# Two half tiles of the output projection moved into the last sample pass, and the sample's loads put in the order of their use

## The chip, the cores and the metric

The kernel runs on one core of a Trainium2 chip, as one program. The metric is the time of one execution on the device in microseconds (us). Before the change it was timed in three runs: 1134.77, 1136.65 and 1139.01, median 1136.65. One more execution was profiled; the times of the views are counted from the start of its span.

## The reference, cut to what matters

One layer of a hybrid decoder works on 512 prompt tokens and 64 sample tokens (8 sequences of 8 new tokens each, with 2048 tokens of past in paged caches). All 576 tokens share the weights.

```python
o_a = nsa(...)    # sparse attention; for the sample: compressed, 16 selected 64-token blocks, window
o_b = hgrn2(...)  # gated linear recurrence
m = ma * (o_a @ w_branch[:512]) + mb * (o_b @ w_branch[512:])   # the merge
x = x + m @ w_out                                               # the output projection
h = rms_norm(x); a, b = split(h @ ffn_w_in); x = x + (silu(conv(a)) * b) @ ffn_w_out
```

`ma` and `mb` are sigmoid gates of 1024 columns each. Everything is float32. The kernel splits each operand of its large products into a high part of fewer bits and the rest (`split`: a cast on ScalarE, a subtraction on VectorE or GpSimd) and adds three products (high by high, high by rest, rest by high), so a weight tile of 128 x 1024 costs 24 matmuls for each half of the tokens. A half is 288 columns (`HF`): the first holds prompt tokens 0 to 287, the second the other prompt tokens and the 64 sample tokens.

## The kernel before, in words

The stages follow each other in `main`: the recurrence and the projections, then `prompt` (attention of the prompt, the gates and the part of the merge that comes from `o_b`), then `sample`, `merge`, `out_proj` and `ffn`. The program is traced in this order and a scheduler gives every engine its own instructions in a fixed order; `issue_after` ties an instruction behind another of its engine. An engine executes its queue in that order and waits at an instruction whose operands aren't there. Tiles of one `tag` share a few buffers, and a load into a buffer waits until the tile before it has been read.

`sample` goes over the 8 sequences in four passes of two (`pr` 0 to 3). A pass needs 32 pages of the cache, 128 KB each: four "halves" of 8 pages (`half`), two for each sequence. Ten buffers hold halves (`NS`), so halves 10 to 15 reuse buffers of earlier ones. A pass also needs a window of keys (`wk`, 512 KB) and one of values (`wv`, 512 KB); four buffers with the tag `nraw` hold these. All these loads, and the loads of weights, stand in the queue of SyncE (SP). The addresses of the pages are read from a table, 8 at a time, and each page is a DMA of its own.

In the code, a pass does the scores of the new keys and the window (`scores_new`, L1569), the exponentials on ScalarE (`softmax_cached`, `softmax_window`), two tiles of the merge's first half (`fill("A")`, `merge_half`, below), the transposes of the probabilities to keys by queries (`by_key`; the copies out of PSUM are ScalarE's for even and VectorE's for odd quarters, L1616 and L1618), the products with the values (`av`, L1624), of which the window's are the last, and then the sum `t1`, its transpose (L1699) and the copies into `oa` (L1704). The next pass's scores (`scores`, L1548) lie between. Loads stand in the program where their buffer comes free: halves 10 and 11 after the second quarter of pass 0, halves 12 and 13 after the fourth, then the values' window of pass 1 (L1677) and the keys' window of pass 2 (L1679).

`merge_half(d)` makes tile `d` (128 of the 1024 columns) of the merge for the first half of the tokens: it loads the gates (`zm`, from the DRAM tile `gbd`, on GpSimd's queue) and the weight `wBr` (SP's queue), splits the weight, runs 12 matmuls (L1346), multiplies and adds on VectorE (L1347) and GpSimd (L1348), and stores the result to `gbd` on GpSimd's queue (L1349). Passes 0 to 3 run tiles 0 and 1, 2 and 3, 4 and 5, 6 and 7. The loads of a pair of tiles stand behind the merges of the pair before, and their splits (`prepare`) behind `t1` of the pass before, ahead of its copies into `oa`.

`merge` loads the eight stored tiles of the first half again (`mb`), splits them into `m`, starts the first output tile with its first half (`begin_out(0)`: 24 matmuls, L1746), splits `oa` into `oas`, and for each of eight tiles loads the gates (`tm`), splits a weight, runs 12 matmuls (L1736) for the second half, multiplies, adds and splits the result into `m` (L1737, L1738, L1739). Then comes the first half of output tile 1 (`begin_out(1)`). `out_proj` runs the second half of these two tiles (L1746) and the other six whole (`gemm`, L378).

## Time and profile before

| | us |
|---|---|
| median of three runs | 1136.65 (1134.77 to 1139.01) |
| the profiled execution, its own time | 1137.31 |
| its span, first to last instruction | 1135.6 |
| TensorE busy | 1072.9 |
| VectorE busy | 745.9 |
| GpSimd busy | 517.1 |
| ScalarE busy | 487.6 |
| mean granted clock of TensorE | 0.978 |

The execution's own time is 1.7 us above its span. PE is TensorE's matmul, PEld its weight load, DVE VectorE, ACT ScalarE, POOL GpSimd, SP SyncE. Matmuls are pipelined, so a busy PE need not be at its peak; the time between the starts of equal matmuls tells their cost. [...] A wait is put down to what ended it last. The sample lies between some 547 and 648 us of the span, the merge between 649 and 683, the whole output tiles behind that.

### The profile page before, as it was taken

The page shows a single profiled execution, that of the slowest core. Times are in us where ns is not written, and L with a number is a line of the kernel's source. Part 1 is how long each engine was busy: PE and PEld are TensorE (multiplying, and loading weights), DVE is VectorE, ACT ScalarE, POOL GpSimd, SP SyncE. Part 2 cuts the span into 40 slices and gives each one's busy share as a digit, 9 for nine tenths or more (in the row PEclk, how much of TensorE's full clock was granted, in tenths as well). Part 3 has the DMA queues.
Part 4 walks back from the last instruction along what each step waited for, and adds up shares of the span by engine and source line. Part 5 has one row for each costly group of instructions (what it writes and reads, how often), then busy time and mean ns, then how long its engine had stood idle before and what let it go on. Part 6 is the DMA issues. An engine that isn't in the chain of part 4 may idle for free.

```text
span 1135.6 us, 21797 instructions
## 1 busy us (share of the span) xinstructions
PE 1072.9 (94%) x7968; PEld 1012.2 (89%) x7968; DVE 745.9 (66%) x1322; ACT 487.6 (43%) x1015; POOL 517.1 (46%) x590
## 2 busy tenths in 40 slices
PE   6999999999999899999985799999999999999998
PEld 5988889898999899989753589999999999999997
DVE  6667665674267757897632484576877868677783
ACT  5523443443444467776522444433343324333341
POOL 3663623832365444333220264354566645554553
PEclk8999999999999899999996999999999999999999
DMA  5633556454341331173688576422364314643223
GB/s 192 184 110 124 158 167 196 127 156 150 113 159 59 127 93 59 53 243 111 218 277 266 184 268 198 123 69 63 115 216 124 101 40 135 210 120 93 69 75 125
DMA packets 106957, 160.98 MB, mean 142 GB/s; under 512 B 11745, under 2 KB 68834, under 8 KB 106722
## 3 DMA queue, kind: packets, MB, share of 16 engines
q1 hardware_dynamic: 105394, 155.40, 43.9%
q0 software_dynamic: 1024, 3.54, 1.0%
q8 instruction: 63, 1.03, 0.4%
q10 hardware_dynamic: 432, 0.65, 0.2%
q14 instruction: 44, 0.36, 0.1%
HBM read 136.34 MB, written 27.33 MB: 144 GB/s over the span
## 4 chain that ended last, share of the span: by engine, by line
PE 45%; DVE 11%; DMA 4%; POOL 4%; issue 3%; SPq 2%; ACT 2%; DVEq 0%; POOLq 0%; ACTq 0%
PE ps_g L378 25%; PE ps_g L1854 7%; PE ps_g L1213 2%; PE ps_po L1624 2%; DVE w L327 2%; PE ps_hp L1320 1%; SPq L943 1%; PE ps_sb L1312 1%; PE ps_sa L1280 1%; POOL rr L1141 1%; DVE r L1151 1%; PE ps_sc L1548 1%; DVE wsp L327 1%; PE ps_tr L1613 1%; DVE g L327 1%
## 5 line engine op out<-in xcount | busy, mean ns | idle before, releaser
L378 PE MATMUL ps_g<-h,w 128*128 128x288 f32 x2112 | 281.0, 294 | 0.0
L378 PEld LDWEIGHTS ps_g<-h,w 128*128 128x128 f32 x2112 | 279.9, 188 | 0.1
L378 PE MATMUL ps_g<-xg,wsp 128*128 128x288 f32 x1200 | 184.1, 306 | 16.0 <-ACT wsp L326 9.3
L378 PEld LDWEIGHTS ps_g<-xg,wsp 128*128 128x128 f32 x1200 | 169.0, 194 | 22.4 <-ACT wsp L326 9.5
L326 ACT CAST w<-wraw 128x512 fp32r<-128x512 f32 (+1 forms) x140 | 84.3, 609 | 141.7 <-PE ps_g L378 98.6
L1854 PE MATMUL ps_g<-g,w 128*128 128x288 f32 x924 | 126.1, 296 | 4.7 <-DVE vv L1887 3.1
L1854 PEld LDWEIGHTS ps_g<-g,w 128*128 128x128 f32 x924 | 123.3, 188 | 6.6 <-DVE vv L1887 4.0
L327 POOL TENSOR_TENSOR w<-wraw,w 128x512 fp32r<-128x512 f32 (+1 forms) x58 | 80.8, 1397 | 52.7 <-ACT w L326 50.3
L327 DVE TENSOR_TENSOR w<-wraw,w 128x512 fp32r<-128x512 f32 (+1 forms) x82 | 76.3, 932 | 23.2 <-ACT w L326 19.6
L326 ACT CAST wsp<-wraw 128x1024 fp32r<-128x1024 f32 (+2 forms) x66 | 58.0, 893 | 62.2 <-DMA wraw<-in_wBr 21.2
L327 DVE TENSOR_TENSOR wsp<-wraw,wsp 128x1024 fp32r<-128x1024 f32 (+2 forms) x43 | 57.0, 1328 | 23.9 <-ACT wsp L326 22.3
L327 POOL TENSOR_TENSOR wsp<-wraw,wsp 128x1024 fp32r<-128x1024 f32 (+2 forms) x23 | 46.9, 2039 | 56.3 <-ACT wsp L326 56.3
L541 PE MATMUL ps_t<-wsp,xg 128*128 128x262 f32 (+1 forms) x480 | 60.9, 286 | 0.0
L541 PEld LDWEIGHTS ps_t<-wsp,xg 128*128 128x128 f32 x480 | 58.9, 189 | 0.1
L1168 POOL TENSOR_TENSOR zg<-zg,rsb 128x576 f32<-128x576 f32 x16 | 25.7, 1606 | 58.4 <-ACT zg L1167 58.4
L916 PE MATMUL ps_pc<-phi,w 128*128 128x256 f32 x256 | 50.8, 289 | 0.0
L326 ACT CAST phi<-praw 128x2048 fp32r<-128x2048 f32 x16 | 30.4, 1901 | 47.4 <-PE ps_pc L916 30.4
L327 DVE TENSOR_TENSOR plo<-praw,phi 128x2048 fp32r<-128x2048 f32 x14 | 32.7, 2338 | 22.2 <-ACT phi L326 14.2
L326 ACT CAST w<-wsum 128x512 fp32r<-128x512 f32 (+1 forms) x48 | 27.7, 584 | 44.6 <-PE ps_g L378 19.8
L327 DVE TENSOR_TENSOR w<-wsum,w 128x512 fp32r<-128x512 f32 (+1 forms) x48 | 41.9, 875 | 6.4 <-ACT w L326 6.1
L1964 POOL TENSOR_TENSOR Y<-Y,rs 128x576 f32<-128x576 f32 x22 | 32.2, 1464 | 25.8 <-ACT Y L1963 25.6
L916 PEld LDWEIGHTS ps_pc<-phi,w 128*128 128x128 f32 x256 | 41.7, 194 | 0.8 <-issue 0.8
(444 smaller groups left out, 2145.0 us busy)
## 6 DMA issues: line engine op xcount, KB each, us to landing
wraw<-in_wFi SPq DMA_DIRECT2D x44, 512.0 KB
praw<-in_pc SPq DMA_DIRECT2D x256, 64.0 KB
praw<-in_pkv SPq DMA_DIRECT2D x96, 128.0 KB
wraw<-in_wM SPq DMA_DIRECT2D x16, 512.0 KB
wraw<-in_wFo SPq DMA_DIRECT2D x16, 512.0 KB
gbd<-zg SPq DMA_DIRECT2D x24, 288.0 KB
wraw<-in_wBr SPq DMA_DIRECT2D x24, 256.0 KB
x<-in_xT SPq DMA_DIRECT2D x16, 288.0 KB
```

The lines of the kernel that those rows point to most:

```text
L326: self.copied = nc.scalar.copy(hi, src)
L327: (eng or nc.vector).tensor_tensor(lo, src, hi.bitcast(F32), op=ALU.subtract)
L378: self.last = nc.tensor.matmul(ps[:, h, 0:HF], w[wk // 4][:, cw, wk % 4] if isinstance(w, list) else w[:, cw, wk, :], (x[cx] if isinstance ...
L541: nc.tensor.matmul(ps[:, 0:n], self.xg[cx][:, k, j * 128:j * 128 + 128], w[k][:, cw], start=(k == 0 and c == 0), stop=(k == KT - 1 and c = ...
L916: self.nc.tensor.matmul(ps, self.w1[:, cw, j, k], x[cx][:, k], start=start and k == 0 and n == 0, stop=k == 7 and n == 2, skip_group_check ...
L943: self.page_dma = nc.sync.dma_start(raw[:, i], dram[bass.ds(rv[i], 1)].rearrange("o p c -> p (o c)"))
L1141: nc.gpsimd.tensor_tensor(rr[0:r, 0:nh], ss[0:r, 0:nh], self.mhalf[0:r, 0:nh], op=ALU.pow)
L1168: nc.gpsimd.tensor_tensor(z, z, self.rsb, op=ALU.mult)
L1213: self.last = nc.tensor.matmul(ps, w[:, cw, k], self.obs[cx][:, k, c], start=n == 0, stop=n == 11)
L1624: self.last = self.nc.tensor.matmul(s.po[64 * bb:64 * bb + 64, branch], pt[:, 64 * bb:64 * bb + 64], v[bb], start=s.first[bb], stop=False, ...
L1854: self.last = nc.tensor.matmul(ps, w[:, cw, j], g[j][:, cx, x], start=first and j == 0 and (cw, cx) == (0, 0), stop=j == m - 1 and (cw, cx ...
L1964: nc.gpsimd.tensor_tensor(s, s, self.rs2, op=ALU.mult)
```

## The change

The diff does the following.

- In `sample`, halves 6 and 7 are loaded, then the values' window of pass 1, then halves 8 and 9. In the passes, the keys' window of pass `pr` + 2 is loaded behind the second quarter and its halves (in pass 0 ahead of halves 12 and 13), and the values' window of pass `pr` + 2 behind the last product of pass `pr`.
- In pass 3, `early_m` takes over four page buffers and one new tile: for `m`'s first half (eight tiles, `mf`) and the weights of output tiles 0 and 1 (`wf`), which are loaded into two window buffers and split on ScalarE and GpSimd. Tiles 0 to 5 of `m` are loaded from `gbd` into the buffer of an earlier pass's scores and split after the second quarter; tiles 6 and 7 are split from the result of `merge_half` in SBUF.
- `begin_out(0)` stands behind the last product of pass 3, `begin_out(1)` behind the transpose of its `t1`. Each copies its PSUM bank to SBUF on ScalarE and stores it to DRAM (`begun`).
- In `merge`, the weights of tiles 0 and 1 come through the ring of the stage before (`ring0`); the other tiles' splits aren't tied behind the last copy of the sample any more; `m`'s first half is loaded and split behind tiles 3 and 4.
- `out_proj` loads and splits the weights of tiles 0 and 1 again, runs their second half, loads `begun` and adds it to `x` on GpSimd.

```diff
@@ -394,6 +394,7 @@
             nc.scalar.dma_start(self.small, self.a["small"])
             self.obd = self.dp.tile([4, 128, T], F32, name="obd")
             self.gbd = self.dp.tile([KT, 128, 2, T], F32, name="gbd")
+            self.begun = self.dp.tile([NE, 128, HF], F32, name="begun")
             self.x2d = self.dp.tile([KT, 128, T], F32, name="x2d")
             self.y2d = self.dp.tile([len(CHUNKS), KT, 128, T], F32, name="y2d")
             self.main()
@@ -445,6 +446,7 @@
         xg.__exit__(None, None, None)
         kc.__exit__(None, None, None)
         mp = self.pool("mp")
+        self.ring0 = self.ring
         with self.banks("psF", g=(2, 4)), self.pool("ringF", 3) as self.ring:
             self.mp = mp.__enter__()
             self.nraw = 4
@@ -1347,6 +1349,8 @@
         nc.vector.scalar_tensor_tensor(z[:, 0], z[:, 0], 1.0, ps, op0=ALU.add, op1=ALU.mult)
         nc.gpsimd.tensor_tensor(z[:, 1], z[:, 1], z[:, 0], op=ALU.add)
         getattr(nc, MSQ).dma_start(self.gbd[d][:, 1, 0:HF], z[:, 1])
+        if d >= 6:
+            self.split_early(d, z[:, 1])
         yield
 
     def first_half(self, r):
@@ -1642,6 +1646,8 @@
             self.halves_to(q, 6)
             wv[0] = self.window_raw(q, self.a["wv"][0])
             self.kw[1] = self.window_raw(q, self.a["wk"][1])
+            self.halves_to(q, 8)
+            wv[1] = self.window_raw(q, self.a["wv"][1])
             self.halves_to(q, NS)
             if FHI < 4:
                 self.first_half(range(FHI, 4))
@@ -1652,12 +1658,17 @@
             for pr in range(4):
                 s = nxt
                 psw = self.scores_new(q, s)
+                if pr == 3:
+                    self.early_m(q, p)
                 self.softmax_cached(s)
                 self.softmax_window(s, psw)
                 s.po = self.bank("po")[:, 0:384].rearrange("p (a b) -> p a b", a=3)
                 self.fill(f"A{pr}")
                 if pr < 3:
                     nxt = self.pair_start(p, pr + 1)
+                else:
+                    mb = p.tile([128, 2688], F32, name="mb0", tag="sS", bufs=2)[:, 0:6 * HF].rearrange("p (d c) -> p d c", d=6)
+                    nc.sync.dma_start(mb, self.gbd[0:6, :, 1, 0:HF].rearrange("d p c -> p d c"))
                 pts = {}
                 with self.tc.issue_after(self.last.ins) if MBK else nullcontext():
                     for x in range(MBK):
@@ -1667,16 +1678,17 @@
                     pt = pts[x] if x in pts else self.key_cached(p, s, x)
                     with self.tc.issue_after(self.last.ins) if x == 0 else nullcontext():
                         self.av_cached(s, pt, x)
+                    if pr == 3 and x == 1:
+                        for d in range(6):
+                            self.split_early(d, mb[:, d])
                     if x in NXT and pr < 3:
                         with self.tc.issue_after(self.last.ins):
                             for y in NXT[x]:
                                 self.scores(q, nxt, y)
                     if x % 2:
                         self.halves_to(q, min(16, NS + 4 * pr + x + 1))
-                if pr < 3:
-                    wv[pr + 1] = self.window_raw(q, self.a["wv"][pr + 1])
-                if pr < 2:
-                    self.kw[pr + 2] = self.window_raw(q, self.a["wk"][pr + 2])
+                        if x == 1 and pr < 2:
+                            self.kw[pr + 2] = self.window_raw(q, self.a["wk"][pr + 2])
                 pt = self.by_key(p, [self.pc[:, pr], s.S[:, 2048:2176]])
                 self.av(s, 2, pt[:, 0], [self.vcf[:, pr, bb] for bb in range(2)])
                 for b in range(2):
@@ -1685,7 +1697,11 @@
                 self.keyed_last = self.copied
                 for i in range(4):
                     self.av(s, 1, pt[:, i], [wv[pr][:, bb, i * 128:i * 128 + 128] for bb in range(2)])
+                if pr < 2:
+                    wv[pr + 2] = self.window_raw(q, self.a["wv"][pr + 2])
                 self.fill(f"C{pr}")
+                if pr == 3:
+                    self.begin_out(0, p)
                 t1 = p.tile([128, 128], F32, name="t1", tag="t1", bufs=2)
                 V.tensor_scalar(t1, s.po[:, 0], s.rr[:, 0:1], None, op0=ALU.mult)
                 V.scalar_tensor_tensor(t1, s.po[:, 1], s.rr[:, 1:2], t1, op0=ALU.mult, op1=ALU.add)
@@ -1706,7 +1722,35 @@
                 if pr < 3:
                     with self.tc.issue_after(self.last.ins):
                         self.scores(q, nxt, 3)
+                else:
+                    with self.tc.issue_after(self.last.ins):
+                        self.begin_out(1, p)
         self.tap("oas", self.oa[:, :, 512:576])
+
+    def early_m(self, q, p):
+
+        part = lambda t, n, c: t[:, 0:2 * n * c].rearrange("p (a n c) -> p a n c", a=2, n=n)
+        room = lambda: q.tile([128, 2048], F32R, name="pm", tag="praw", bufs=NS - 4)
+        self.mf = [part(room(), n, HF) for n in (3, 3, 2)]
+        self.wf = [part(t, KT, 128) for t in (room(), p.tile([128, 2048], F32R, name="wf1"))]
+        for d in range(NE):
+            raw = q.tile([128, KT, 128], F32, name="wf0", tag="nraw", bufs=NRAW)
+            self.nc.sync.dma_start(raw, self.a["wO"][d])
+            for i in (0, 4):
+                self.split(self.wf[d][:, 0, i:i + 4], self.wf[d][:, 1, i:i + 4], raw[:, i:i + 4], eng=self.nc.gpsimd)
+
+    def split_early(self, d, src):
+        self.split(self.mf[d // 3][:, 0, d % 3], self.mf[d // 3][:, 1, d % 3], src, scale=0.5)
+
+    def begin_out(self, d, p):
+
+        ps = self.bank("sc")[:, 0:HF]
+        todo = [(k, t) for k in range(KT) for t in THREE]
+        for n, (k, (cw, cx)) in enumerate(todo):
+            self.last = self.nc.tensor.matmul(ps, self.wf[d][:, cw, k], self.mf[k // 3][:, cx, k % 3], start=n == 0, stop=n == len(todo) - 1)
+        out = p.tile([128, HF], F32, name="bo", tag="pt", bufs=3)
+        self.nc.scalar.copy(out, ps)
+        self.nc.sync.dma_start(self.begun[d], out)
 
 
     def merge(self):
@@ -1714,44 +1758,35 @@
         V = nc.vector
         self.m = self.mp.tile([128, 2, KT, T], F32R, name="m")
         self.pool_every = MPE
-        self.begun = []
         with self.pool("mg") as p:
-            for d, n in MBG:
-                mb = p.tile([128, n, HF], F32, name="mb0", tag=f"mb{d}")
-                getattr(nc, MBQ).dma_start(mb, self.gbd[d:d + n, :, 1, 0:HF].rearrange("d p c -> p d c"))
-                for i in range(n):
-                    self.split(self.m[:, 0, d + i, 0:HF], self.m[:, 1, d + i, 0:HF], mb[:, i], scale=0.5)
-            self.begin_out(0)
             oas = p.tile([128, 2, 4, HF], F32R, name="oas")
+            ring, self.ring, self.nraw = self.ring, self.ring0, None
+            ready = [self.wsplit(a["wBr"][d][:, 0:4], 4, 128) for d in range(2)]
+            self.ring, self.nraw = ring, 4
             for i in range(4):
                 self.split(oas[:, 0, i], oas[:, 1, i], self.oa[:, i, HF:T])
             for d in range(KT):
                 tm = p.tile([128, 2, HF], F32, name="tm", tag="tm", bufs=TMB)
                 getattr(nc, MQ).dma_start(tm, self.gbd[d].rearrange("p a (b c) -> p b a c", b=2)[:, 1])
                 ps = self.bank("g")[:, 0, 0:HF]
-                w = self.wload(a["wBr"][d][:, 0:4], 4, 128)
-                with self.tc.issue_after(self.keyed_last.ins):
-                    w = self.wsplit(None, 4, 128, (p, "wm", WMB), raw=w)
+                w = ready[d] if d < 2 else self.wsplit(a["wBr"][d][:, 0:4], 4, 128, (p, "wm", WMB))
                 for n, (k, (cw, cx)) in enumerate((k, t) for k in range(4) for t in THREE):
                     nc.tensor.matmul(ps, w[:, cw, k], oas[:, cx, k], start=n == 0, stop=n == 11)
                 V.scalar_tensor_tensor(tm[:, 0], tm[:, 0], 1.0, ps, op0=ALU.add, op1=ALU.mult)
                 nc.gpsimd.tensor_tensor(tm[:, 1], tm[:, 1], tm[:, 0], op=ALU.add)
                 self.split(self.m[:, 0, d, HF:T], self.m[:, 1, d, HF:T], tm[:, 1], scale=0.5)
-            for d in range(1, NE):
-                self.begin_out(d)
+                if d in (3, 4):
+                    c, n = MBG[d - 3]
+                    mb = p.tile([128, n, HF], F32, name="mb0", tag=f"mb{c}")
+                    getattr(nc, MBQ).dma_start(mb, self.gbd[c:c + n, :, 1, 0:HF].rearrange("d p c -> p d c"))
+                    for i in range(n):
+                        self.split(self.m[:, 0, c + i, 0:HF], self.m[:, 1, c + i, 0:HF], mb[:, i], scale=0.5)
 
     def out_half(self, ps, w, h):
         todo = [(k, t) for k in range(KT) for t in THREE]
         for n, (k, (cw, cx)) in enumerate(todo):
             self.last = self.nc.tensor.matmul(ps[:, h, 0:HF], w[k // 4][:, cw, k % 4], self.m[:, cx, k, h * HF:h * HF + HF],
                                               start=n == 0, stop=n == len(todo) - 1)
-
-    def begin_out(self, d):
-
-        w = self.whalves(self.a["wO"][d])
-        ps = self.bank("g")
-        self.out_half(ps, w, 0)
-        self.begun.append((ps, w))
 
     def out_proj(self):
 
@@ -1763,18 +1798,23 @@
         with self.pool("op", 2, "right") as p:
             acc = self.acc = self.fp.tile([128, T], F32, name="acc")
             for d in range(KT):
+                w = self.whalves(a["wO"][d])
+                ps = self.bank("g")
                 if d < NE:
-                    ps, w = self.begun[d]
                     self.out_half(ps, w, 1)
                 else:
-                    w = self.whalves(a["wO"][d])
-                    ps = self.bank("g")
                     self.gemm(ps, [(w, range(KT), self.m, range(KT))])
                 x = p.tile([128, T], F32, name="x", tag="x")
                 nc.sync.dma_start(x, a["xT"][:, d])
                 x2 = p.tile([128, T], F32, name="x2", tag="x2", bufs=3)
-                V.tensor_tensor(x2.rearrange("p (a b) -> p a b", a=2), ps[:, :, 0:HF],
-                                x.rearrange("p (a b) -> p a b", a=2), op=ALU.add)
+                if d < NE:
+                    bo = p.tile([128, HF], F32, name="bo", tag="bo")
+                    nc.sync.dma_start(bo, self.begun[d])
+                    nc.gpsimd.tensor_tensor(x2[:, 0:HF], bo, x[:, 0:HF], op=ALU.add)
+                    V.tensor_tensor(x2[:, HF:T], ps[:, 1, 0:HF], x[:, HF:T], op=ALU.add)
+                else:
+                    V.tensor_tensor(x2.rearrange("p (a b) -> p a b", a=2), ps[:, :, 0:HF],
+                                    x.rearrange("p (a b) -> p a b", a=2), op=ALU.add)
                 nc.sync.dma_start(self.x2d[d], x2)
                 self.split(self.h2[:, 0, d], self.h2[:, 1, d], x2, scale=self.small[:, 8 + d:9 + d])
                 if d == 0:
```

## Rows read from the trace of the kernel before

**Rows 1.** The page, part 1: busy us, share of the span, instructions.

```profile
PE 1072.9 (94%) x7968; PEld 1012.2 (89%) x7968; DVE 745.9 (66%) x1322; ACT 487.6 (43%) x1015; POOL 517.1 (46%) x590
```

**Rows 2.** Waits of all engines, 540 to 700 us: total, times, longest.

```profile
PE ps_po L1624 <- DMA nraw<-in_wv: 15.9, 1, 15.9
```

**Rows 3.** Stretches: us, busy us of each engine, TensorE's granted clock, DMA share, GB/s.

```profile
600.00:610.00 10.00, 0.28 (x4) 0.31 (x6) 0.00 (x0) 0.00 (x0) 0.00 (x0) 0.50 0.87 261
610.00:620.00 10.00, 9.87 (x57) 6.03 (x55) 5.32 (x19) 5.15 (x12) 0.75 (x1) 0.73 0.93 286
632.00:639.00 7.00, 6.91 (x49) 5.63 (x48) 4.47 (x18) 4.50 (x11) 1.84 (x3) 1.00 0.00 0
646.50:683.00 36.50, 28.05 (x193) 27.18 (x194) 29.16 (x44) 19.79 (x46) 20.55 (x17) 0.91 0.80 272
```

**Rows 4.** SyncE's queue in order of time: start, us to the last issue.

```profile
586.75 9.53 SPq L943 DMA_DIRECT2D pgs<-in_pkv  x16
597.11 8.71 SPq L943 DMA_DIRECT2D praw<-in_pkv  x16
605.87 0.43 SPq L1438 DMA_DIRECT2D nraw<-in_wv  x1
...
606.87 0.84 SPq L334 DMA_DIRECT2D wraw<-in_wBr  x2
608.54 9.68 SPq L943 DMA_DIRECT2D praw<-in_pkv  x16
```

**Rows 5.** The chain that ended last, 570 to 580 us: start us, us, what.

```profile
573.00 3.81 DMA praw<-in_pkv
```

**Rows 6.** Order of time, 578 to 625 us: start, us, engine, line [idle, releaser].

```profile
609.72 1.98 PE L1624 MATMUL ps_po<-nraw,pt 128*64 128x128 f32 x16 [15.87 <-DMA nraw<-in_wv]
...
611.78 1.34 ACT L326 CAST wsp<-wraw 128x512 fp32r<-128x512 f32 x2 [18.06 <-DMA wraw<-in_wBr]
...
616.79 1.82 PE L1346 MATMUL ps_sm<-oas,wsp 128*128 128x288 f32 x12
```

**Rows 7.** Order of time, 625 to 700 us: the sample's end, the merge.

```profile
645.34 1.09 PE L1624 MATMUL ps_po<-nraw,pt 128*64 128x128 f32 x16
...
647.69 0.30 PE L1699 MATMUL ps_tr<-c_base,t 128*128 128x128 f32 x1 [1.26 <-DVE t L1692]
...
649.29 1.56 DVE L327 TENSOR_TENSOR oas<-oa,oas 128x288 fp32r<-128x288 f32 x4 [1.74 <-ACT oas L326]
...
653.25 0.61 PE L1746 MATMUL ps_g<-m,w 128*128 128x288 f32 x1 [5.25 <-ACT m L329]
...
660.37 7.22 PE L1736 MATMUL ps_g<-oas,wsp 128*128 128x288 f32 x53
...
683.00 17.21 PE L378 MATMUL ps_g<-m,w 128*128 128x288 f32 x128
```

**Rows 8.** Order of time, 655 to 662 us: one merge tile's chain.

```profile
658.33 0.44 DVE L1737 SCALAR_TENSOR_TENSOR tm<-tm,ps_g 128x288 f32<-128x288 f32 x1
...
660.16 0.46 DVE L330 SCALAR_TENSOR_TENSOR m<-tm,m 128x288 fp32r<-128x288 f32 x1 [1.39 <-ACT m L329]
```

**Rows 9.** VectorE's groups, 646.5 to 683 us: busy us, mean ns, idle before.

```profile
L327 DVE TENSOR_TENSOR w<-wraw,w 128x512 fp32r<-128x512 f32 x8 | 8.4, 1063 | 1.8 <-ACT w L326 1.3 <-DMA mb<-gbd 0.5
...
L330 DVE SCALAR_TENSOR_TENSOR m<-tm,m 128x288 fp32r<-128x288 f32 x8 | 6.9, 878 | 3.6 <-ACT m L329 3.6
...
L327 DVE TENSOR_TENSOR wsp<-wraw,wsp 128x512 fp32r<-128x512 f32 x4 | 5.1, 1278 | 0.0
...
L330 DVE SCALAR_TENSOR_TENSOR m<-mb,m 128x288 fp32r<-128x288 f32 x8 | 4.1, 582 | 0.0
```

**Rows 10.** Order of time; a DMA's issues, last its median us to landing.

```profile
639.65 0.57 POOL L1349 DMA_DIRECT2D gbd<-zm  x1 [0.30 <-POOL zm L1348]
...
640.84 0.69 DVE L1618 COPY pt<-ps_tr 128x512 f32<-128x512 f32 x1 [0.85 <-PE ps_tr L1613]
...
gbd<-zm POOLq DMA_DIRECT2D x8, 144.0 KB, 4.3
```

## The prediction

> **What bounds the kernel now.** I read the page's engine totals first: TensorE is busy 94% of the 1135.6 us span [rows 1], so only TensorE's idle time can be won, and only where it idles. Then the waits of the stretch that the diff touches. One row says that the window product of a sample pass waited 15.9 us for its V window [rows 2]. [...] The SyncE queue in order of time gives the reason. Thirty-two pages of later passes (586.75 to 605.82) stand ahead of that window, which is issued at 605.87 only [rows 4] and is used at 609.72 [rows 6]. The second hole is behind the sample: the last window product ends at 646.43, one transpose runs at 647.69, and the next matmul is at 653.25, after 5.25 us of waiting for a split of m [rows 7].
>
> **Part one: the loads.** A page costs SyncE 8.71/16 = 0.54 us of issue and a window 0.43 us [rows 4]. So the window of pass 1, put ahead of halves 8 and 9, delays the pages behind it by 0.43 us. Its own landing is bounded by 3.81 us [rows 5] and 3.85 us (605.87 to 609.72); issued some 30 us earlier it is early by far, and the 15.9 us wait goes. What is late next? I follow the queue. Halves 10 and 11: last issue 596.28 + 0.43, landing 3.8 later, 600.5. The K window of pass 2, next in the queue, lands near 601. So TensorE finishes pass 1 and stands at pass 2's first merge matmuls (L1346) near 602. These need the weights of tiles 4 and 5. Their loads come behind halves 12 and 13 in program order, and that is the order in which the queue now issues them (606.87) [rows 4]. Two windows are still ahead of them beside those pages, and now a third (V of pass 2), so the issue moves from 606.87 to 607.3. With 0.5 MB less right in front (at the 286 GB/s of 610 to 620 [rows 3], 1.7 us of data) I let them land at 611.0; ScalarE's cast of them now begins at 611.78, after an 18 us wait [rows 6]. A cast of 0.67 [rows 6] and a subtraction of between as much and 1.28 [rows 9] give a first merge matmul at 612.3 to 613, against 616.79 now [rows 6].
>
> So 15.9 us of wait shrink to some 4.3 us of gain, since the wait takes another name. [...] I charge 1.7 and book 2.6 us. The ends are 0 (weights no earlier) and 10 (weights ahead of the pages; then halves 14 and 15, issued from 608.5 to 618.2 [rows 4] and landing 3.8 later, are the next limit).
>
> **Part two: the early half products.** Before, tile 0 and tile 1 of W_out take 2 x 24 matmuls for the first 288 columns inside the merge; 24 x 0.136 = 3.3 us each [rows 7]. They go to the end of the last pass: 3.3 us behind its last product, 3.3 us behind its transpose. Nothing is saved in TensorE work; it fills the hole. Now from 646.43 to the first full product at 683.00 pass 36.6 us [rows 7] for 192 x 0.136 + 0.3 = 26.4 us of work, so at most 10.2 us is to be had. Step by step, in times of the trace: the first half product stands ahead of the transpose, which moves from 647.69 to 649.7 (2.0 late); the copies to oa and the split of oas end at 650.85 + 2.0 = 652.9 [rows 7]. The second half product covers this until 653.3. Its PSUM bank must be copied out before the merge's pool takes it over; I allow 0.6 us. The 96 merge matmuls run 653.9 to 667.0 at a warm clock; the last tile's chain VectorE, GpSimd, ScalarE, VectorE takes 658.33 to 660.62 = 2.3 us [rows 8], 669.3; three matmuls left of tile 0, then 24 of tile 1: 673.0. That would be a gain of 10.0.
>
> VectorE has a say. Of 36.5 us it is busy 29.2 [rows 3]. What must be done before the full products: 1.2 for t1 and the hand-over, oas 1.6 [rows 7], three of the six weight splits at 1.28 (3.8), eight subtractions m<-tm 6.9, eight m<-mb 4.1, four W_out halves at 1.06 (4.2) [rows 9], eight products into tm at 0.44 (3.5) [rows 8]: 25.3 us, and about 3 us in which it must wait for oas and the first bank. 646.4 + 28.3 = 674.7. I take 676, between that and the present 683: a gain of 7. Its ends are 2 (VectorE stretched) and 10.
>
> **What is added.** Four casts (0.67 each [rows 6]) and four GpSimd subtractions of the two W_out tiles, eight casts and eight subtractions of m (the latter 4.1 us [rows 9]), two copies, two stores, two W_out loads, a 864 KB load of m, later two loads of the stored half and two GpSimd additions. They fall into the last pass; over 632 to 639 ScalarE is busy 4.5 of 7 us, VectorE 4.5, GpSimd 1.8 and the DMA engines not at all [rows 3], so the room is there. On ScalarE and VectorE they share in-order queues with the copies that TensorE waits for: between 0 and 3 us, I take 1, the nearer end, since the loads have an idle DMA to themselves. The W_out tiles are loaded and split a second time in the projection; this is in the 25.3 us. The full products behind 683 are one unbroken run and only start earlier.
>
> **Sum.** 2.6 + 7 - 1 = 8.6 us on the profiled execution's 1137.31 gives 1128.7; the median before is 1136.65, 0.7 lower, so I say 1128.5. Less than 0.5% (5.7 us: 1131.0 to 1142.3) counts as no change here.
>
> **Rivals.**
> *VectorE becomes the bound of the merge.* For: its subtraction on 288 columns takes 0.878 us on the mean in the stretch for m<-tm, but 0.582 for m<-mb [rows 9], so it is stretched where GpSimd runs. Against: it still has 7 us idle [rows 3]. If 18 us of GpSimd work squeezed into 27 instead of 36 us stretch the 25.3 us by a fifth, the full products start at 679.5, and 2.6 + 3.5 - 1 gives 1132. [...]
>
> [...]
>
> *Part one is worth 10.* The weights' loads pass the pages: 1120.5. Against: the present queue keeps program order.
>
> *The m load lands late, and the time gets longer.* The six splits of m stand in the queues ahead of the copies of the pass's second half (VectorE's is at 640.84 [rows 10]). If the load has to wait for the last merge's store (issued at 639.65 now, 2.6 sooner then, landing 4.3 us later [rows 10]: 641.4) and then takes 5 (864 KB; my estimate from a window's 3.85 for 512 KB), six splits of 0.58 end near 650.3, the copy comes 12 us late, the pass restarts at half clock and ends near 659, and with the steps of part two behind that the full products begin near 686 or 687 instead of 683: 1141. It decides from a landing later than about 640.5. Against: the tiles that it reads, 0 to 5, are stored a pass earlier, and the DMA engines are idle from 632 on [rows 3].
>
> *It doesn't do what it says*, the half products find the splits unready and run where they did: with part one alone 1134.5.
>
> **Chances.** Forecast 0.50 (own range 1125 to 1131.5); VectorE bound 0.14; changed name 0.09; part one in full 0.08; late load 0.10; not as it says 0.06; unseen 0.03. Range 1121 to 1139. Faster by over 0.5%: 0.46 of the forecast, 0.08, and 0.08 of the two cases around 1132: 0.62. Slower by over 0.5%: 0.06 of the late load and the 0.03: 0.09. The rest, 0.29.
>
> **What would show it.** Right: no wait for the V window; a TensorE gap near 602 to 612 that ends on the weights of tiles 4 and 5; matmuls of the half products back to back from the last pass into the merge, at full clock; merge matmuls without other products between; full products near 674 in the old times, less 2.6. Wrong: the gap near 602 missing or longer than 12 us, VectorE without idle time in the merge, or TensorE waiting inside the last pass for a copy behind a split of m.

## The result, and the profile after

The changed kernel takes 1151.49 us (median of four runs, 1147.98 to 1154.15) against 1136.44 for the kernel before beside it: ratio 1.0127, 95% interval 1.0108 to 1.0147. It is 1.3% slower, where I forecast 1128.5 and a range of 1121 to 1139. The profiled execution took 1154.15 us, its span 1152.4.

Page of after, part 1 (busy us, share, instructions), against [rows 1]: for the same 7968 matmuls TensorE is busy 13.2 us longer. Much of the loss does not show as waiting but as longer products, and the granted clock, a share of full speed, is lower where they run (0.86 against 0.91 up to the sample's last product).

```profile
PE 1086.1 (94%) x7968; PEld 1021.0 (89%) x7968; DVE 746.6 (65%) x1331; ACT 491.8 (43%) x1029; POOL 521.7 (45%) x595
```

Stretches of after, as [rows 3] (us, busy us of PE, PEld, DVE, ACT, POOL, granted clock, DMA share, GB/s): from the prompt's last product to the sample's last one, then to the full products. Before, the first took 90.49 us with 71.69 busy at a clock of 0.91, the second 36.57. The first now holds 16 of the 24 matmuls of the first half product, 2.2 us at 0.136 each.

```profile
557.41:663.97 106.56, 82.84 (x663) 58.66 (x662) 39.28 (x116) 33.61 (x74) 23.86 (x29) 0.86 0.70 218
663.97:696.20 32.23, 26.74 (x179) 25.01 (x178) 21.36 (x39) 17.01 (x42) 14.56 (x14) 0.95 0.83 277
```

Order of time of after, TensorE (start, us, line, [idle, releaser]), against [rows 6, 7]:

```profile
603.00 1.09 PE L1628 MATMUL ps_po<-nraw,pt 128*64 128x128 f32 x16
621.29 3.49 PE L1348 MATMUL ps_sm<-oas,wsp 128*128 128x288 f32 x12 [11.11 <-ACT wsp L326]
624.59 2.90 PE L1348 MATMUL ps_g<-oas,wsp 128*128 128x288 f32 x12
...
649.31 1.84 PE L1617 MATMUL ps_tr<-c_base,sS 128*128 128x128 f32 x12 [2.17 <-ACT sS L1596]
652.04 1.12 PE L1617 MATMUL ps_tr<-c_base,sS 128*128 128x128 f32 x4 [0.89 <-DVE pt L1622]
653.09 3.68 PE L1628 MATMUL ps_po<-praw,pt 128*64 128x128 f32 x32
...
657.04 1.54 PE L1750 MATMUL ps_sc<-pm 128*128 128x288 f32 x7
...
658.77 0.64 PE L1750 MATMUL ps_sc<-pm 128*128 128x288 f32 x3
...
661.90 1.05 PE L1750 MATMUL ps_sc<-pm 128*128 128x288 f32 x6
662.88 1.09 PE L1628 MATMUL ps_po<-nraw,pt 128*64 128x128 f32 x16
663.91 1.32 PE L1750 MATMUL ps_sc<-pm 128*128 128x288 f32 x8
...
665.23 3.43 PE L1750 MATMUL ps_sc<-pm,wf 128*128 128x288 f32 x24
...
684.55 1.31 PE L1774 MATMUL ps_g<-oas,wsp 128*128 128x288 f32 x4 [4.36 <-ACT wsp L326]
...
690.12 4.96 PE L1788 MATMUL ps_g<-m,w 128*128 128x288 f32 x36
```

The products of the last pass that took 3.68 us took 1.97 before:

```profile
640.66 1.97 PE L1624 MATMUL ps_po<-praw,pt 128*64 128x128 f32 x32
```

The V window is no longer waited for (603.00, before 609.72 after 15.87 us). The wait has another name, 11.11 us for the weights of tiles 4 and 5. The last pass has waits and a restart at the lower clock (granted 0.50 from 653.0 to 656.7), and the first half product does not stand behind the last product as planned: its matmuls run in four pieces (x7, x3, x6, x8), 16 of them inside the pass. The merge waits 4.36 us for a weight split. SyncE's queue (total, times, longest) has two long waits that before does not have:

```profile
SPq L1753 <- ACT oa L1720: 23.9, 1, 23.9
SPq L304 <- DVE oa L1333: 5.3, 1, 5.3
```

The first is the store of a half product, the second the load of the sample's constants. The table counts from the start of the last product of the prompt (555.94 us before, 557.41 after), so that variation ahead of the sample is left out. "Full" is the start of the unbroken run of full products, less 0.13 us for each full product that ran between other ones before it; "rest" is what follows to the span's end. All numbers are differences of times in the order of time. Each row is one execution: e7 and e13 are the same kernel and differ by up to 2.3 us in a column, while the steps from one column to the next agree within 0.1 us from pass 3 on.

| kernel | merges of pass 0 start | of pass 2 | of pass 3 | last product ends | full | rest |
|---|---|---|---|---|---|---|
| before | 4.7 | 60.8 | 78.4 | 90.5 | 127.1 | 452.6 |
| after | 8.9 | 63.9 | 86.3 | 106.6 | 138.8 | 456.2 |
| e1 loads alone | 4.7 | 58.2 | 78.5 | 90.6 | 126.9 | 452.1 |
| e3 constants on GpSimd's queue | 8.1 | 61.5 | 82.1 | 99.0 | 133.1 | 452.0 |
| e5 stores on ScalarE's queue | 8.8 | 63.2 | 84.9 | 102.7 | 133.1 | 452.4 |
| e7 loads and weights, no halves | 4.7 | 49.5 | 72.1 | 84.2 | 120.3 | 451.8 |
| e13 the same again | 4.7 | 50.1 | 74.4 | 86.5 | 122.5 | 451.8 |
| e8 all queue edits, halves | 8.9 | 49.9 | 72.3 | 93.1 | 124.4 | 452.0 |
| e10 e8 and W_out splits later | 8.9 | 46.7 | 70.5 | 86.0 | 117.6 | 452.9 |
| e11 the same, on VectorE | 8.9 | 48.8 | 73.4 | 88.8 | 120.6 | 453.2 |
| e12 e10 and m's splits last | 9.1 | 49.3 | 71.9 | 87.4 | 118.5 | 452.5 |

So of 16.8 us of span, 7.9 are lost up to the merges of pass 3, 8.2 in the last pass, 4.4 are won in the merge, 1.5 lie ahead of the sample and 3.6 behind it. The last is hardly the change's: with the same code behind the merge e3 and e5 have 452.0 and 452.4, and this execution was the slowest of its four.

### The profile page after: what moved, and what is told of

Its sections match the earlier page's. It is cut to its first block, busy times and chain, and to the rows that moved or that the text cites. A ratio compares the mean times of both kernels' runs of the same rounds, so it can differ in the third digit from the quotient of the medians.

```text
span 1152.4 us, 21863 instructions
## 1 busy us (share of the span) xinstructions
PE 1086.1 (94%) x7968; PEld 1021.0 (89%) x7968; DVE 746.6 (65%) x1331; ACT 491.8 (43%) x1029; POOL 521.7 (45%) x595
## 4 chain that ended last, share of the span: by engine, by line
PE 47%; DVE 10%; DMA 5%; POOL 3%; ACT 3%; issue 2%; SPq 1%; DVEq 0%; POOLq 0%; ACTq 0%
PE ps_g L378 25%; PE ps_g L1894 7%; PE ps_g L1215 2%; PE ps_hp L1322 2%; PE ps_sb L1314 2%; DVE w L327 1%; PE ps_sa L1282 1%; DMA wf<-in_wO 1%; PE ps_po L1628 1%; DMA praw<-in_pkv 1%; PE ps_sc L1552 1%; POOL rr L1143 1%; DVE r L1153 1%; SPq L945 1%; DVE g L327 1%
## 5 line engine op out<-in xcount | busy, mean ns | idle before, releaser
L1894 PE MATMUL ps_g<-g,w 128*128 128x288 f32 x924 | 127.1, 298 | 7.2 <-DVE y L1940 3.2
```

Source lines behind the costliest of these rows:

```text
L1894: self.last = nc.tensor.matmul(ps, w[:, cw, j], g[j][:, cx, x], start=first and j == 0 and (cw, cx) == (0, 0), stop=j == m - 1 and (cw, cx ...
```

## The experiments

**e1, e2: the two parts alone.** e1 is the kernel before with part one, e2 the changed kernel with the loads in their old order.

```diff
 e1, on the kernel before (e2, on the changed kernel, has the same lines, + and - exchanged)
+self.halves_to(q, 8)
+wv[1] = self.window_raw(q, self.a["wv"][1])
...
-if pr < 3:
-    wv[pr + 1] = self.window_raw(q, self.a["wv"][pr + 1])
-if pr < 2:
-    self.kw[pr + 2] = self.window_raw(q, self.a["wk"][pr + 2])
+if x == 1 and pr < 2:
+    self.kw[pr + 2] = self.window_raw(q, self.a["wk"][pr + 2])
...
+if pr < 2:
+    wv[pr + 2] = self.window_raw(q, self.a["wv"][pr + 2])
```

> The kernel before with part one only (V window of pass 1 ahead of halves 8 and 9, the K windows of passes 2 and 3 and the V windows of passes 2 and 3 in the new places); the half products stay in the merge. Theory (the loss is in part two and in what it does to SyncE's queue; the loads by themselves are worth a little): 1131 to 1136 us, the wait for the V window gone (603 instead of 609.7 us), the next merges of the sample held by the weights of tiles 4 and 5 until about 613, nothing changed in the last pass. Rival (the new load order itself costs, by moving pages behind windows): 1140 us or more, with pages 4 to 7 or the later halves late.

> The changed kernel with the loads in their old order: the early half products alone. Theory: slower by 12 to 20 us than the kernel before (1149 to 1156), with the sample's constants held on SyncE's queue by about 5 us near 551 to 560, the V window of pass 1 waited for again, and the last pass longer by some 8 us. Rival (the loads cost, the half products gain): about 1130 us.

e1: 1135.76 against 1136.59, ratio 0.9994 [0.9974, 1.0014], no difference. e2: 1155.31, 1.0157 [1.0133, 1.0181]. The loss is part two's; part one is worth nothing by itself. Order of time of e1:

```profile
611.99 3.50 PE L1346 MATMUL ps_sm<-oas,wsp 128*128 128x288 f32 x12 [10.24 <-ACT wsp L326]
615.29 2.66 PE L1346 MATMUL ps_g<-oas,wsp 128*128 128x288 f32 x12
```

The prediction put the start of these merges at 612.3 to 613. That 611.99 is so near is luck: the prompt's last product starts 2.1 us earlier in this execution (553.83 against 555.94), so in the times of before it is 614.1. Counted from the prompt the merges start 2.6 us earlier than before (58.2 against 60.8), but the 24 products take 5.8 us instead of 3.3 (in after, behind a wait of 11.11 us, they take 6.0 at a granted clock of 0.52, 621.29 to 627.40), and at pass 3 nothing is left (78.5 against 78.4).

**e3, e9: the constants' load.** e3 is the changed kernel with one queue altered; e9 the kernel before with an unused tile in the place of the new one.

```diff
 e3:
-self.load_consts(p, "sample")
+self.load_consts(p, "sample", nc.gpsimd)
 e9:
+spare = p.tile([128, 2048], F32R, name="wf1")     # pr == 3
+nc.gpsimd.memset(spare[:, 0:1].bitcast(F32), 0.0)
```

> The changed kernel with one edit: the load of the sample's constants is issued on GpSimd's queue instead of SyncE's. Theory: the constants' new place in memory makes their load wait 5.3 us for a VectorE instruction of the prompt's last head, and the pages behind it on SyncE's queue wait with it; off that queue, pages 4 and 5 start near 554 again and the first merges near 561 to 563 instead of 566: 1143 to 1148 us. Rival (the pages are late for another reason, or the delay is taken up by the later wait for weights anyway): 1150 to 1153 us, the first merges near 566 or the second pass where it was.

> The kernel before with an 8 KB tile more in the sample's pool on the right, in which one column is set and nothing else done: the place that the changed kernel gives the second tile of W_out. Theory (placement alone holds the constants' load): SyncE waits some 5 us for a VectorE instruction of the prompt's last head before it issues the constants, the pages behind it come 5 to 7 us later, the first merges near 566 instead of 560.6, and since the V window's load stands behind the same pages the whole sample is late by about as much: 1141 to 1145 us. Rival (placement is harmless, something else in the changed kernel held the load): 1135 to 1138 us, first merges near 561.

e3: 1143.98, 7.5 us less than the changed kernel, 1.0063 [1.0041, 1.0084]. e9: 1141.97 against 1136.64, 1.0034 [1.0015, 1.0054]: 8 KB that nobody uses cost 4 to 5 us. SyncE's waits in e9:

```profile
SPq L304 <- DVE oa L1331: 6.4, 1, 6.4
```

With a tile in the place of `wf1` in the pool, the constants' load waits 6.4 us for the last VectorE instruction of the prompt's last head, and the pages queued behind it wait too. The wait says that the constants now lie on memory which that head still uses; the addresses themselves were not read. In e3 the first merges stay late (8.1), but what comes behind the pages is earlier than in after, by 2.4 us at pass 2 and 4.2 at pass 3.

**e4, e16: the W_out splits in the changed kernel.** e4 puts load and split of tile 1 behind the exponentials in program order; e16 ties the splits of both tiles behind ScalarE's third copy of pass 3.

```diff
 e4:                                  e16:
 self.softmax_window(s, psw)          +if pr == 3 and x == 2:
+if pr == 3: self.early_w(q, 1)       +    with self.tc.issue_after(self.copied.ins):
                                      +        self.early_w()
```

> The changed kernel with one edit: the load and the split of the second tile of W_out stand behind the exponentials of the last pass in program order, instead of ahead of them. Theory: on ScalarE the two casts of that tile held the exponentials of the last pass by 4.3 us (648.0 instead of 643.7); behind them, the last pass runs 3 to 5 us shorter and the kernel takes 1146 to 1149 us. Rival (the splits of m and the cold clock are what lengthens the last pass): under 1.5 us shorter, 1150 to 1152.

> The changed kernel with one edit, and none of the queue edits: the splits of the two W_out tiles are tied behind ScalarE's copy of the third quarter of the last pass, so that on ScalarE the exponentials stand ahead of them, and GpSimd's four subtractions come behind its additions for the merges. Theory (late W_out load, casts ahead of the exponentials, subtractions beside VectorE's product): the exponentials follow the scores at once (within 1 us instead of 4.3), the product of rr and grow takes 2 us or less, the last pass is 4 to 6 us shorter: 1145 to 1148 us. Rival (the pass is long because of the splits of m, which now stand ahead of both copies): 1150 to 1153 us.

e4: 1148.25, 1.0091 [1.0061, 1.0121], within the theory's numbers, but it tells nothing of the theory: the scheduler left the casts ahead of the exponentials. e16: 1146.62, 1.0091 [1.0059, 1.0124], within the theory's numbers too and yet not for its reason. (Both intervals overlap that of the changed kernel.) The exponentials follow at once, but the pass is no shorter (22.2 us from the merges to the last product; 20.3 in after), because now the six splits of m stand ahead of a copy on VectorE:

```profile
646.27 4.45 DVE L330 SCALAR_TENSOR_TENSOR pm<-mb,pm 128x288 fp32r<-128x288 f32 x6
650.64 1.75 DVE L327 TENSOR_TENSOR wsp<-wraw,wsp 128x512 fp32r<-128x512 f32 x1
652.31 0.68 DVE L1622 COPY pt<-ps_tr 128x512 f32<-128x512 f32 x1
```

TensorE waits 3.0 us for that copy, and 2.1 us for the one before it. The order is the rival's, but the six take 4.45 us, 0.74 each on the mean; in after six took 2.36 us, 0.39 each. The casts of the W_out tiles, which GpSimd's subtractions follow, lie in the same stretch (646.65 to 648.84); that these subtractions stretch the splits is not shown. Nor does e16's profile win anything up to the full products (140.5 against 138.8 in after): what it is faster by lies ahead of the sample and in the rest (451.8).

**e5: the stores.**

```diff
-self.nc.sync.dma_start(self.begun[d], out)
+self.nc.scalar.dma_start(self.begun[d], out)
```

> The changed kernel with one edit: the two finished half products are stored from ScalarE's queue, right behind the copies that make them, instead of from SyncE's. Theory: on SyncE the first of these stores waited 23.9 us for its half product, and the merge's loads of weights and gates stood behind it; off that queue they are issued some 20 us earlier, the merge loses its 4.4 us wait for a weight split and most of the waits for m, and the full products of the output projection begin 4 to 8 us earlier: 1143.5 to 1147.5 us. Rival (the merge is bound by VectorE or by the order of ScalarE's splits, the loads were only late because nothing needed them): 1149.5 to 1153 us, the wait for the split still there.

1143.94, 1.0063 [1.0037, 1.0088], 7.5 us less. Behind the waiting store stood the merge's loads: five weight loads are issued from 637.37 to 655.16 in e5; in after one came at 641.63 and the next at 666.19. The 4.4 us wait for a split is 2.0. The table puts the gain of its profile (5.7 at "full") in several places: 1.4 before pass 3, 2.5 in the last pass, 1.8 in the merge. Only the 1.8 lie behind the store in time. Up to there SyncE's queue has the same order in both, and most of the 2.5 is that the 32 products that took 3.68 us in after take 1.97 here. So the store costs time, but that it alone costs all of the 7.5 us is not shown.

**e7, e13: the weights past the pages.** Part one on the kernel before, and one constant; no half products. e13 is e7 a second time, beside e12.

```diff
-MWQ = "sync"
+MWQ = "gpsimd"
```

> The kernel before with the new order of loads (part one) and one word more: the weights of the merges inside the sample are loaded from GpSimd's queue instead of SyncE's, so that they don't stand behind pages. No half products. Theory: the wait for the V window then goes without taking another name; the third pair of merges starts near 602 to 604 us instead of 612 (part one alone) and 616.8 (before), and the kernel takes 1125 to 1129 us. Rival (the next pages, halves 12 to 15, become the wait): 1131 to 1135 us, with waits of some 5 us for pages behind 605 us.

> The loads in the new order with the merges' weights on GpSimd's queue, no half products, a second time beside the run with the splits of m last. Theory: 1125 to 1129 us as in the first run, and 0 to 3 us slower than its neighbour, so that the half products are worth no more than that even with every queue cleared. Rival: the half products are worth the 7 us that were forecast, 1129 us or more beside 1124 or less.

e7: 1126.78, 0.9906 [0.9872, 0.9940]; e13: 1128.29, 0.9917 [0.9892, 0.9941]. Faster than both kernels. Order of time of e7:

```profile
602.24 1.85 PE L1346 MATMUL ps_sm<-oas,wsp 128*128 128x288 f32 x12
603.93 1.77 PE L1346 MATMUL ps_g<-oas,wsp 128*128 128x288 f32 x12
```

No wait and no restart at a lower clock (1.00 from 600 to 610). These are the 10 us that the prediction had as its far end of part one, with the next limit where it had it: of the 11.3 us that e7's profile is ahead of before at pass 2, 6.3 are left at pass 3, with a wait for the last pages.

```profile
620.38 1.04 PE L1548 MATMUL ps_sc<-praw,Qs 128*64 128x512 f32 x2 [2.74 <-DMA praw<-in_pkv]
```

The rival, pages as the next wait, is there too, but smaller than it said. No run has the weights' queue alone, without part one, so whether the gain needs both is open.

**e8: all three queue edits with both parts** (e3, e5 and e7's edit in the changed kernel).

> The changed kernel, both parts, with the three queue edits together: constants of the sample and weights of its merges loaded from GpSimd's queue, half products stored from ScalarE's. Theory (what the change lost, it lost behind waiting instructions of in-order queues, and the half products are worth something once these are gone): 1121 to 1127 us, 3 to 6 us less than the loads with the weights alone. Rival (the half products with their extra splits are worth nothing here, as the merge is bound by VectorE): 1127 to 1132 us, no better than the loads with the weights alone.

1133.51, 0.9979 [0.9957, 1.0001], 18 us less than the changed kernel, yet 6.7 more than e7. My theory was wrong here: the queues are not all. The last pass takes 20.8 us from the merges to the last product, 12.1 in e7. VectorE, GpSimd and TensorE in e8:

```profile
630.20 4.56 DVE L1609 TENSOR_TENSOR rr<-rr,grow 128x2 f32<-128x2 f32 x1
634.68 0.68 DVE L1622 COPY pt<-ps_tr 128x512 f32<-128x512 f32 x1
```

```profile
630.27 0.81 POOL L1350 TENSOR_TENSOR zm<-zm 128x288 f32<-128x288 f32 x1
631.02 2.49 POOL L327 TENSOR_TENSOR pm<-wf,pm 128x512 fp32r<-128x512 f32 x2
633.47 1.26 POOL L327 TENSOR_TENSOR wsp<-wraw,wsp 128x512 fp32r<-128x512 f32 x1
```

```profile
635.41 1.12 PE L1617 MATMUL ps_tr<-c_base,sS 128*128 128x128 f32 x4 [4.56 <-DVE pt L1622]
636.46 4.87 PE L1628 MATMUL ps_po<-praw,pt 128*64 128x128 f32 x48
```

A product of two columns takes 4.56 us and ends with GpSimd's last subtraction (634.73); the copy behind it is late by as much, and TensorE restarts slowly (the 48 products take 4.87 us, in e16 2.84).

**e10, e11: e8 with the W_out splits behind the last quarter,** on GpSimd or on VectorE.

```diff
+if pr == 3 and x == 3:
+    self.early_w()        # e10: eng=nc.gpsimd, e11: eng=nc.vector
```

> The kernel with all three queue edits, and one more: the splits of the two W_out tiles (casts on ScalarE, subtractions on GpSimd) stand behind the last quarter of the last pass instead of ahead of its exponentials. Theory: a VectorE instruction with two inputs in SBUF is held while GpSimd's subtractions run (the product of rr and grow, two columns, took 4.56 us beside them and 0.15 with GpSimd idle); behind it stood the copy that TensorE waited 4.6 us for. With GpSimd's work moved away that product takes under 1 us, the wait is gone, the last pass is 4 to 6 us shorter: 1127 to 1130 us. Rival (the casts and splits of m that are queued ahead of the copies make the last pass long): 1132 to 1135 us, the copy as late as before.

> As the run with the W_out splits behind the last quarter, but their subtractions on VectorE instead of GpSimd (4 x 0.7 us where VectorE is idle for 5 us). Theory: the same end of the last pass or up to 1.5 us earlier, as nothing of GpSimd is left to hold VectorE: 1126 to 1129 us, about as fast as the loads with the weights alone (1126.8) or faster. Rival (VectorE has no room there, the chain behind the last product is late): 1130 to 1133 us.

1128.81, 0.9941 [0.9920, 0.9961], and 1130.03, 0.9935 [0.9911, 0.9960]. The product takes 2.13 us in e10 (beside an addition and one subtraction on GpSimd) and 2.14 in e11, the wait for the copy is 0.53 in both, the last pass 15.5 and 15.4 us. That is 3.3 to 3.4 more than e7's 12.1: 15 (e10) and 20 (e11) of the 24 matmuls of the first half product now lie in it, 2.0 and 2.7 us at 0.136, beside that wait and, in e10, one of 0.32 for a split of m.

**e14, e15: GpSimd's work by itself,** in e7, on a tile of its own, tied behind GpSimd's last addition for the merges.

```diff
+nc.gpsimd.tensor_tensor(extra_i, extra_i, extra_i, op=ALU.subtract)   # e14: x4, 512 columns
+nc.gpsimd.memset(extra, 0.0)                                         # e15: x4, 2048 columns
```

> The loads in the new order with the merges' weights on GpSimd's queue, no half products, and four GpSimd subtractions of 512 columns on a tile of their own, put right behind GpSimd's last addition for the merges of the last pass (their result is not used; the tile is set to zero earlier by GpSimd). Theory (VectorE's instructions with two inputs in SBUF are held while GpSimd's subtractions run): the product of rr and grow takes 5 us or more instead of 0.9, ends when GpSimd's last subtraction ends, the copy behind it is late, TensorE waits 3 to 5 us: 1130 to 1134 us. Rival (the casts and loads of the half products did it): the product under 1.5 us, 1126 to 1129 us.

> As the run with four GpSimd subtractions, with four GpSimd memsets of 2048 columns in their place (some 2 us each, estimated from 0.52 us for 512 columns): work without a read from SBUF, for as long or longer. Theory (it is subtractions, which read SBUF, that hold VectorE): the product of rr and grow under 1.5 us, 1126 to 1129 us. Rival (any work on GpSimd holds VectorE): the product takes 5 us or more, 1130 us or more.

e14: 1134.53, 6 to 8 us over e7 and e13. e15: 1127.68, none. e14, GpSimd, VectorE and TensorE, then e15:

```profile
631.13 4.02 POOL L1351 TENSOR_TENSOR extra<-extra 128x512 f32<-128x512 f32 x4
```

```profile
630.29 4.88 DVE L1608 TENSOR_TENSOR rr<-rr,grow 128x2 f32<-128x2 f32 x1
635.09 1.28 DVE L1621 COPY pt<-ps_tr 128x512 f32<-128x512 f32 x2
```

```profile
635.83 3.59 PE L1627 MATMUL ps_po<-praw,pt 128*64 128x128 f32 x32 [3.27 <-DVE pt L1621]
```

```profile
629.30 1.80 POOL L1351 MEMSET extra<- 128x2048 f32 x1
```

```profile
628.58 0.79 DVE L1608 TENSOR_TENSOR rr<-rr,grow 128x2 f32<-128x2 f32 x1
```

With subtractions the product lasts until 635.17, the end of the fourth (635.15). With memsets it ends at 629.37, with GpSimd's addition (628.57 to 629.36), though the first memset follows without a gap. No cast and no load is needed for the effect.

**e12: the splits of m last in the merge,** on e10, tied behind the last weight cast.

```diff
+with self.tc.issue_after(last_w.ins):
     for c, n, mb in mbs: ...   # the eight splits m<-mb
```

> The kernel with the three queue edits and the W_out splits behind the last quarter, and one more: inside the merge the eight splits of m's first half stand behind the last weight casts on ScalarE instead of ahead of the last two. Theory: the merge's waits of 3.2 and 0.6 us for the last weight splits go, full products begin some 3 us earlier against the start of the last pass, 1124 to 1127 us. Rival (VectorE, which does those subtractions anyway, bounds the merge): 1128 to 1130 us, the wait taken by m.

1128.93, 0.9931 [0.9911, 0.9952], as e10 and as e13 beside it (1128.29). The rival's number, not its reason: the waits for the last weights shrink from 3.8 to 2.4 us and are now for their loads, and the first full products run in pieces (18 of them ahead of the unbroken run). So part one with the weights on GpSimd's queue (e7, e13) is faster than both kernels, and the half products add nothing to it that these runs resolve.

## Why the prediction was wrong, step by step

Three steps failed, and with them the sign. The stores that part two adds, and the load that its new tile makes late, were given no wait in SyncE's queue. The cost in the last pass was put at 1 us and was 6.0. Part two's 7 us rested on half products that end early in the merge; even with the queues cleared about 1 us of them came. In the prediction's own terms, +2.6, -1 and +7 became, in the profile, -7.9 up to pass 3, -8.2 in the last pass and +4.4 in the merge. (A slip of the sum decides nothing: 1128.7 less 0.7 is 1128.0, not 1128.5.)

**Part one.** The mechanism came as written: the V window's wait gone, a gap that ends on the weights of tiles 4 and 5. Only the size was off: 2.6 was booked as 4.3 less 1.7 for the restart; 2.6 less 2.5 came. No run shows the 1.7: from the first of the 24 products to what follows them pass 5.80 us in e1 and 6.04 in after, against 3.27 before, 2.5 and 2.8 more. Of the chances, "changed name" (0.09) was right about this part: it was worth nothing. "Part one in full" needed the weights to pass the pages, and e7 and e13 show that with part one in place this decides: 9 to 10 us against before.

**What the sum did not have.** I followed SyncE's queue for the loads that were moved, but not for those that were added, and did not ask where the new tile lies. The constants' load (a wait of 5.3 us; 7.5 us of time by e3, 4 to 5 by e9) and the first store of a half product (a wait of 23.9 us; 7.5 us of time by e5, of which its profile shows 1.8 behind the store) wait in that queue ahead of loads that TensorE needs. Neither stood among the terms or the rivals. With the weights' queue, e8 recovers 18 us; the three do not add up separately.

**"Cost in the last pass 1, since the loads have an idle DMA to themselves."** It was 6.0: 8.2 less 2.2 for the 16 matmuls of the half product that ran inside the pass. TensorE's rows above give 5.6 of it, waits of 2.17 and 0.89 us and some 2.5 us more for the transposes and products behind them at the lower clock (0.73 from 649.3 to 653.0, then 0.50). The 2.17 are for the exponentials. The DMA engines were not idle (share 0.50 from 637.83 to 640.34, 0.76 from there to 648), and SyncE could not issue the load of W_out tile 1 until 640.34; by the profile it waited for GpSimd to end tile 0's split (640.32). The casts of tile 1 wait for that load and hold the exponentials until 648.02 on ScalarE:

```profile
SPq L1738 <- POOL pm L327: 1.1, 1, 1.1
637.83 2.49 POOL L327 TENSOR_TENSOR pm<-wf,pm 128x512 fp32r<-128x512 f32 x2 [0.65 <-ACT pm L326]
646.97 1.14 ACT L326 CAST wf<-wf 128x512 fp32r<-128x512 f32 x2 [4.79 <-DMA wf<-in_wO]
648.02 1.14 ACT L1596 ACTIVATE sS<-sS,nm 128x1024 f32<-128x1024 f32 x1
```

The rival that ended slower had this mechanism, a late load whose splits stand ahead of what TensorE waits for, but named m's load, and priced it at 1141 with a chance of 0.10. This is read from the rows; no run took it away by itself (e16 put another split in its place). VectorE's product is stretched in after too, to 1.98 us, but there the copy that TensorE waits for (0.89) stands ahead of it, so no cost of it is seen in after as there is in e8 and e14.

**Part two, 7 us.** In the kernels with the queues cleared and the splits moved (e10, e11, e12), from the last product to the full ones pass 31.1 to 31.8 us against 36.0 and 36.1 in e7 and e13: 4.2 to 5.0 us less. But 15 to 20 matmuls of the first half product lie ahead of that, in the pass, where TensorE had no idle time (in e7 12.09 of 12.10 us busy), and the pass is 3.3 to 3.4 us longer. That leaves 0.8 to 1.6 us, where the prediction had 7 less 1. What follows to the span's end is 0.7 to 1.4 us longer (452.5 to 453.2 against 451.8); e8 has the same code there and 452.0, so whether these belong to the change is open. With them -0.6 to 0.9 us is left, and the medians (1128.8 to 1130.0 against 1126.8 and 1128.3) show no gain. Two steps failed here. One is the place of the first half product: it was to fill the hole behind the last product, and most of it ran where there was none. The other is the merge's end: I let 27 of the 48 second-half products run last, 3.7 us, the others inside the merge. In after 46 of them stand behind the last merge product, 6.3 us, and the merge itself waits for weight casts that are queued behind the splits of m on ScalarE:

```profile
680.55 2.11 ACT L329 ACTIVATE m<-mb 128x288 fp32r<-128x288 f32 x6 [1.82 <-DMA mb<-gbd]
...
683.89 1.12 ACT L326 CAST wsp<-wraw 128x512 fp32r<-128x512 f32 x2
```

**VectorE as the bound.** Not in the merge: in after it is busy 22.36 of the 33.4 us. The line is stretch, its length, then busy us of PE, PEld, DVE, ACT and POOL, the clock, DMA share, GB/s:

```profile
663.80:697.20 33.40, 27.91 (x189) 26.08 (x186) 22.36 (x40) 17.50 (x43) 15.56 (x14) 0.95 0.83 280
```

That VectorE's instructions take longer beside GpSimd's was right, the place wrong: it cost time where a small VectorE instruction stood ahead of a copy that TensorE waited for, in the last pass (e8: a product of 4.56 us, a wait of 4.56). The longer product came with GpSimd's subtractions and not with its memsets: it took 4.88 us beside an addition and four subtractions (e14), and 0.79 beside the addition alone when memsets follow it (e15).

What stays open: whether the cleared half products gain or cost a microsecond, since the medians differ by less than their spread; what e5 gains ahead of the store; and whether the weights' queue would gain as much without part one.

## What to carry to other kernels

For each DMA that a change adds, write down what it waits for and what stands behind it in its queue: a store that waits for a product belongs on the queue of the engine that makes it, not ahead of loads (e5: a wait of 23.9 us gone, 7.5 us less, of which its rows behind the store show 1.8). A new tile in a pool can move its neighbours (e9: a load waits 6.4 us, 4 to 5 us of time); look at which load now waits for the tile that had that memory. Filling a hole with moved products pays only as far as the products really land in it: count those that land in a stretch where the engine was already full (e10 and e11: 15 and 20 of 24), and the splits that come with them.

## What the runs showed of the hardware that was not expected

A VectorE product of two columns with both inputs in SBUF took 0.16 us with GpSimd idle (after, 613.50; none of its instructions that compute lies between 595.3 and 625.4), 0.92 beside one GpSimd addition of 288 columns (before, 638.47; the addition from 638.54 to 639.35), 2.13 beside an addition and one subtraction (e10), and 4.56 and 4.88 beside an addition and three or four subtractions (e8, e14). Each of these took GpSimd 0.8 to 1.3 us, and the product ended with the last of the row (634.76 and 634.73 in e8, 635.17 and 635.15 in e14). With memsets behind the addition, the first of 1.8 us, it ended with the addition (629.37 and 629.36, e15). Splits of 288 columns were longer too: in e10 four splits of m (128 x 288, both inputs in SBUF) took 5.50 us beside four GpSimd subtractions of the W_out tiles, in e11, where VectorE makes these subtractions itself, 1.55 (636.51). That is 1.4 us each on the mean against 0.39.

```profile
634.98 5.50 DVE L330 SCALAR_TENSOR_TENSOR pm<-mb,pm 128x288 fp32r<-128x288 f32 x4
634.52 2.73 POOL L327 TENSOR_TENSOR pm<-wf,pm 128x512 fp32r<-128x512 f32 x2 [1.65 <-ACT pm L326]
637.21 2.95 POOL L327 TENSOR_TENSOR wf<-wf,wf 128x512 fp32r<-128x512 f32 x2
```
